# Two blocks on one core: the mixer's last three output tiles and the first two gate and up tiles in token halves, with token sums on TensorE

## Chip, cores and metric

The kernel runs on one core of one Trainium2 chip. The time is that of one execution on the device in microseconds, launch to end, as the median of several runs. Lower is better.

## What is computed

528 tokens of width 1024 (16 meta tokens and 512 of the sequence) go through a first block: a token mixer (a state-space branch and an mLSTM branch, merged) and a gated FFN with a causal convolution along the tokens. A second block, an attention block with its own FFN, follows on the 512 sequence tokens. The change lies where the first block's mixer ends and its FFN begins. All is float32.

```python
def rmsnorm(x, g):
    xf = x.astype(jnp.float32)
    y = xf * lax.rsqrt(jnp.mean(xf * xf, axis=-1, keepdims=True) + NORM_EPS)
    return (y * g.astype(jnp.float32)).astype(x.dtype)

def token_mixer(x, g_pre, g_post, ...):
    ...
    return x + rmsnorm(merged @ w_out, g_post)

def channel_mixer(x, g_pre, g_post, w_gate, w_up, w_conv, b_conv, w_down):
    h = rmsnorm(x, g_pre)
    a = causal_dwconv(h @ w_gate, w_conv, b_conv)
    y = (jax.nn.gelu(a, approximate=True) * (h @ w_up)) @ w_down
    return x + rmsnorm(y, g_post)
```

## The kernel before

Activations lie with features on the 128 partitions and tokens along the free axis; a tile is one of eight blocks of 128 features. The 528 tokens are held as two halves of HF = 258 tokens, from tokens 14 and 270 on (HEADTOK): 256 that count and two ahead of them, which the convolution needs. Each product is made in three matmuls, for accuracy: operands are split into a high and a low part, and `mm3` (L171 to L179) issues, for each block k of the contraction, high by high, high weight by low activation, low weight by high activation, each for every output half. So a tile of 1024 by 128 weights is 48 matmuls for two halves, and a product whose output is one PSUM bank of 512 columns is 24.

`split_w` (L159 to L169) makes the weights ready: SyncE (SP) loads a raw tile (three buffers), ScalarE (ACT) casts it to the high part `wh` (L167), VectorE (DVE) subtracts to get the low part `wl` (L168). High and low parts have four buffers, two in each of two pools that are used in turn.

The place of the change is the end of `token_mixer` (L457 to L498):

1. Eight output tiles (L463 to L468): 48 matmuls each into `d`, two PSUM banks, one for each half; ScalarE copies them to `y` (L467) and squares the copy (L530); GpSimd (POOL) adds the squares up in `nacc` (L534), the last square stays apart as `nsq`.
2. The norm of the output (L470): a token's sum over partitions is a matmul with a vector of ones (`tok_sum`, L210), 128 tokens at a time, five of them for 516 tokens, for `nacc` and for `nsq`; VectorE makes the root in ten small operations (L217, L185 to L195); six transposes (`bcast_cols`, L223) spread it over all partitions. Between them stand matmuls whose results nobody reads ("spins", L230).
3. The residual pass (L472 to L487): for each tile SP loads the input `xr`, VectorE scales each half (`pt`, L478), an add of the input follows (L481, L486; VectorE for even tiles, GpSimd for odd ones), then `part` splits the result into `xh` (ScalarE, L570) and `xl` (VectorE, L571), and its squares are added up (L530, L534).
4. The first FFN tiles, f = 0 and 1 (`ffn_products`, L488): a gate product `fg` of 48 matmuls of 258 columns, an up product `fm` of 24 matmuls of 512 columns.
5. The sums of the second norm, its root, and transposes into the row `ffn_rstd` (L490 to L497). The FFN loop takes the first two tiles' results out of PSUM with it (L1110 `gs`, L1118 `gt`), and from f = 2 on makes its own products.

Which instruction stands where in an engine's queue is set by a scheduler when the kernel is built; the program text gives it the dependences, and `high_priority` and `issue_after` steer it. PSUM has two pools: `pd`, two tiles of two banks (tag `d`), and `pm`, four tiles of one bank (tag `m`).

## Time and profile before

| | us |
|---|---|
| median of 3 runs | 1474.9 (1471.9 to 1474.96) |
| profiled execution | 1474.1 |
| its span, first to last instruction | 1472.3 |
| TensorE busy | 1433.4 (97%) |
| VectorE busy | 818.8 (56%) |
| ScalarE busy | 637.4 (43%) |
| GpSimd busy | 313.8 (21%) |
| mean granted TensorE clock | 0.990 of full speed |

Busy time is that in which an engine has an instruction under way; matmuls overlap, so it is a share of the span in which TensorE is not idle, and not its peak. Weight loads (PEld) are counted apart, since they lie beside matmuls. A start in the timeline is when an instruction began, and the time behind it how long it, or the whole run of like instructions, took; the distance of two starts is the pace. In brackets stands the idle time of the engine ahead of an instruction and what ended it.

### The profile page before, as it was taken

The page shows a single profiled execution, that of the slowest core. Times are in us where ns is not written, and L with a number is a line of the kernel's source. Part 1 is how long each engine was busy: PE and PEld are TensorE (multiplying, and loading weights), DVE is VectorE, ACT ScalarE, POOL GpSimd, SP SyncE. Part 2 cuts the span into 40 slices and gives each one's busy share as a digit, 9 for nine tenths or more (in the row PEclk, how much of TensorE's full clock was granted, in tenths as well). Part 3 has the DMA queues.
Part 4 walks back from the last instruction along what each step waited for, and adds up shares of the span by engine and source line. Part 5 has one row for each costly group of instructions (what it writes and reads, how often), then busy time and mean ns, then how long its engine had stood idle before and what let it go on. Part 6 is the DMA issues. An engine that isn't in the chain of part 4 may idle for free.

```text
span 1472.3 us, 22643 instructions
## 1 busy us (share of the span) xinstructions
PE 1433.4 (97%) x9050; PEld 1294.6 (88%) x9050; DVE 818.8 (56%) x1463; ACT 637.4 (43%) x1026; POOL 313.8 (21%) x383
## 2 busy tenths in 40 slices
PE   7999988999999999999999899999998999999998
PEld 7999988999998988899988799999886888888887
DVE  8868643544447663256543668888776542244321
ACT  4455555732434332233332447777654532134310
POOL 0019881010124210001111513223454000000000
PEclk9999998999999999999999999999999999999999
DMA  5662212232521322332223133333222322222330
GB/s 177 157 116 77 73 65 55 85 94 74 178 91 68 108 85 79 116 101 87 91 80 96 44 105 112 102 109 107 69 70 92 116 92 100 101 93 93 108 122 29
DMA packets 65892, 140.32 MB, mean 95 GB/s; under 512 B 18806, under 2 KB 30454, under 8 KB 65788
## 3 DMA queue, kind: packets, MB, share of 16 engines
q1 hardware_dynamic: 52672, 129.90, 27.2%
q10 hardware_dynamic: 13116, 8.99, 2.6%
q8 instruction: 71, 1.16, 0.3%
q14 instruction: 33, 0.27, 0.1%
HBM read 128.83 MB, written 4.76 MB: 91 GB/s over the span
## 4 chain that ended last, share of the span: by engine, by line
PE 81%; POOL 9%; DVE 4%; issue 2%; ACT 2%; DMA 2%; ACTq 0%; DVEq 0%; POOLq 0%
PE fm L178 16%; PE d L178 13%; PE mp L178 12%; PE ad L178 9%; PE ad L1196 8%; PE fg L178 8%; PE ad L1407 3%; PE ao L178 3%; POOL ra L808 3%; POOL X L810 2%; POOL rb L809 2%; PE at L1317 1%; PE as L1292 1%; PE ao L1329 1%; DVE wl L168 1%
## 5 line engine op out<-in xcount | busy, mean ns | idle before, releaser
L167 ACT CAST wh<-wr 128x1024 fp32r<-128x1024 f32 (+2 forms) x240 | 232.9, 972 | 533.9 <-PE d L178 103.3
L168 DVE TENSOR_TENSOR wl<-wr,wh 128x1024 fp32r<-128x1024 f32 (+2 forms) x240 | 293.4, 1225 | 204.8 <-ACT wh L167 203.3
L178 PE MATMUL d<-xh,wl 128*128 128x258 f32 (+1 forms) x576 | 121.3, 290 | 1.8 <-DVE wl L168 1.8
L178 PE MATMUL d<-xh,wh 128*128 128x258 f32 (+1 forms) x576 | 121.9, 293 | 0.0
L178 PE MATMUL d<-xl,wh 128*128 128x258 f32 (+1 forms) x576 | 119.1, 288 | 0.0
L1196 PE MATMUL ad<-wh,xh 128*128 128x256 f32 x384 | 111.1, 293 | 2.6 <-ACT wh L167 1.3
L1196 PE MATMUL ad<-wh,xl 128*128 128x256 f32 x384 | 111.2, 291 | 1.4 <-DVE xl L571 1.2
L1196 PE MATMUL ad<-wl,xh 128*128 128x256 f32 x384 | 110.6, 290 | 0.4 <-DVE wl L168 0.4
L178 PEld LDWEIGHTS d<-xh,wl 128*128 128x128 f32 x576 | 91.3, 192 | 4.9 <-issue 2.3
L178 PEld LDWEIGHTS d<-xh,wh 128*128 128x128 f32 x576 | 91.8, 194 | 2.6 <-issue 1.0
L178 PEld LDWEIGHTS d<-xl,wh 128*128 128x128 f32 x576 | 91.0, 193 | 0.4
L1119 POOL TENSOR_TENSOR gt<-gt,ga 128x512 f32<-128x512 f32 x22 | 31.5, 1432 | 267.6 <-ACT wh L167 202.9
L1196 PEld LDWEIGHTS ad<-wh,xh 128*128 128x128 f32 x384 | 74.2, 195 | 3.9 <-ACT xh L570 1.9
L1196 PEld LDWEIGHTS ad<-wh,xl 128*128 128x128 f32 x384 | 74.9, 195 | 2.8 <-DVE xl L571 2.2
L1196 PEld LDWEIGHTS ad<-wl,xh 128*128 128x128 f32 x384 | 74.8, 195 | 1.1 <-DVE wl L168 0.7
L178 PE MATMUL fg<-xh,wh 128*128 128x258 f32 x352 | 71.8, 285 | 1.9 <-ACT xh L570 1.9
L534 POOL TENSOR_TENSOR nacc<-nacc,nsq 128x512 f32<-128x512 f32 (+1 forms) x37 | 53.3, 1440 | 91.7 <-ACT nsq L530 88.3
L178 PE MATMUL fg<-xl,wh 128*128 128x258 f32 x352 | 71.7, 286 | 0.7 <-DVE xl L571 0.7
L178 PE MATMUL fg<-xh,wl 128*128 128x258 f32 x352 | 71.9, 285 | 0.0
L178 PE MATMUL fm<-xh,wh 128*128 128x512 f32 x176 | 70.3, 400 | 0.1
L178 PE MATMUL fm<-xl,wh 128*128 128x512 f32 x176 | 70.3, 400 | 0.0
L178 PE MATMUL fm<-xh,wl 128*128 128x512 f32 x176 | 70.0, 397 | 0.0
(459 smaller groups left out, 3622.3 us busy)
## 6 DMA issues: line engine op xcount, KB each, us to landing
wr<-in_wd_dram SPq DMA_DIRECT2D x48, 512.0 KB
wr<-in_wgu_dram SPq DMA_DIRECT2D x44, 512.0 KB
wr<-in_w_dram SPq DMA_DIRECT2D x36, 512.0 KB
wr<-in_wup_dram SPq DMA_DIRECT2D x32, 512.0 KB
wr<-in_wqkv_dram SPq DMA_DIRECT2D x24, 512.0 KB
wr<-in_wo_dram SPq DMA_DIRECT2D x10, 512.0 KB
wr<-in_wab_dram SPq DMA_DIRECT2D x16, 256.0 KB
wr<-in_wd_dram SPq DMA_DIRECT2D x16, 192.0 KB
```

Of the source, the lines that this page charges most:

```text
L167: nc.scalar.copy(hi[:, :n], raw[:, :n])
L168: (eng or nc.vector).tensor_sub(lo[:, :n], raw[:, :n], hi[:, :n].bitcast(F))
L178: self.mm = self.nc.tensor.matmul(o, a[:, k, :], x(k, p), start=first and k == order[0] and t == 0, stop=last and k == order[-1] and t == 2)
L534: self.eng.tensor_add(self.parts[0], self.parts[0], sq)
L808: P.tensor_tensor(a, self.AR, X[:, :, :, k - 1].unsqueeze(1).to_broadcast([128, 2, 2, G]), op=OP.mult)
L809: P.tensor_tensor(b, a[:, 0], a[:, 1, ::-1], op=OP.add)
L810: P.tensor_tensor(X[:, :, :, k], X[:, :, :, k], b, op=OP.add)
L1119: P.tensor_mul(t, t, a)
L1196: nc.tensor.matmul(o, x[:, k, 128 * tt : 128 * tt + 128], w[:, k4], start=k == 0 and i == 0 and tt % 2 == 0, stop=k == 7 and i == 2, skip_ ...
L1292: nc.tensor.matmul(ps[:, b:e], q, kl[:, :n], start=False, stop=True, skip_group_check=True)
L1317: nc.tensor.transpose(pt[:, e : e + 128], p[:, off[i] + 128 * j : off[i] + 128 * j + 128], c.idn)
L1407: nc.tensor.matmul(ps, x[:, k], y[:, k, :S], start=i == 0 and t == 0, stop=i == kt - 1 and t == 2)
```

## The change

Of the eight mixer output tiles, five stay as they are. The last three are made half by half: all three tiles of the first token half, then all three of the second, from the same weights, which stay in their buffers (`ws`). Each half tile is copied, and squared straight from PSUM, on ScalarE. The square of each half tile goes to TensorE by itself: `TokSums.add` issues three sums of 128 tokens (tokens 0, 128 and 130 on) which accumulate in PSUM; the five whole tiles' sum of squares joins them with six sums. The root and the transposes are made for each half.

The residual pass runs by halves too (`residual`): eight tiles of the first half, then eight of the second. Squares of the halves go to TensorE one by one, or in pairs which GpSimd adds first (m = 1, 3, 5); the tiles 1, 3, 5, 6 and 7 give three sums each.

The first two gate and up tiles (`ffn_half`) are made by halves: gate 0, up 0, gate 1, up 1 for the first half, tile by tile; for the second half all four go side by side, k by k. Their four weights stay until the last k. Up products have 256 columns for each half in place of 512. The spins are left out here.

In the sums, L559 of the changed kernel is the matmul of `TokSums.add`, 54 in all: 6, 9 and 9 for the first norm, 15 and 15 for the second.

```diff
-        post = PostNorm(c, op, 2 * HF)
-        for m in range(8):
+        rr = c.xp.tile([128, 2, HF], F, name="ffn_rstd", tag="rrow")
+        thirds = (0, 128, HF - 128)
+
+        def spread(cols):
+            ps = misc()
+            c.bcast_cols(cols, [(j, ps[:, s : s + 128]) for j, s in enumerate(thirds)])
+            return ps[:, :HF]
+
+        def square(x):
+            sq = op.tile([128, HF], F, name="hsq", tag="hsq", bufs=4)
+            A.activation(sq, x, AF.Square)
+            return sq
+
+        post = PostNorm(c, op, 2 * HF, 5, direct=0)
+        for m in range(5):
...
-        pa, pb = misc(), misc()
-        post.finish(misc(), [pa, pb], spins=(4, 8, 6), idle=misc())
+        ws = [c.split_w(I["wo1"][m], 1024) for m in range(5, 8)]
+        sums = TokSums(c, misc())
         pre = PreNorm(c, op, 2 * HF, "g_ffn_pre", 0)
-        for m in range(8):
-            xr = op.tile([128, 2, HF], F, name="xr", tag="xr", bufs=4)
...
-        c.first = [ffn_products(c, f) for f in range(2)]
-        with tc.high_priority():
-            ffn_rstd = pre.finish(misc(), (0, 128, 256, 384, 388))
...
+        def residual(p):
+            for m in range(8):
+                xr = op.tile([128, HF], F, name="xr", tag="xr", bufs=6)
+                nc.sync.dma_start(xr, I["hT"][m][:, HEADTOK[p] : HEADTOK[p] + HF])
+                t = op.tile([128, HF], F, name="pt", tag="pt", bufs=2)
+                V.scalar_tensor_tensor(t, y[:, m, p], c.v("g_mix_post", m), rs[p], op0=OP.mult, op1=OP.mult)
+                (P if m % 2 else V).tensor_add(y[:, m, p], t, xr)
+                pre.part(m, y[:, m], slice(p, p + 1))
+                sq = square(y[:, m, p])
+                if m in (1, 3, 5):
+                    P.tensor_add(sq, sq, last)
+                last = sq
+                if m not in (0, 2, 4):
+                    sums.add(6 + 3 * p, sq, thirds, m == 7)
+
+        def row(p):
+            with tc.high_priority():
+                A.copy(rr[:, p], spread(sums.finish(6 + 3 * p, 3)))
+
+        for p in range(2):
+            if p == 0:
+                sums.add(0, post.parts[0], [HF * q + s for q in range(2) for s in thirds], False)
+            for m in range(5, 8):
...
+                c.mm3([ps], ws[m - 5], 8, lambda k, _: mgh[:, k, p], lambda k, _: mgl[k][:, p])
+                A.copy(y[:, m, p], ps)
+                sums.add(3 * p, square(ps), thirds, m == 7)
+            rs.append(spread(sums.finish(3 * p, 3)))
+            if p == 0:
+                first_weights = [c.split_w(I["wgu"][0, 0], 1024)]
+        residual(0)
+        first_weights += [c.split_w(I["wgu"][f, j], 1024) for f, j in ((0, 1), (1, 0), (1, 1))]
...
+        for j in range(4):
+            outs.append(misc() if j % 2 else c.pd.tile([128, 2, 512], F, name="fg", tag="d"))
+            ffn_half(c, first_weights[j], outs[j], j % 2, 0)
+        row(0)
+        residual(1)
+        for k in range(8):
+            for j in range(4):
+                ffn_half(c, first_weights[j], outs[j], j % 2, 1, (k,))
+        row(1)
...
+class TokSums:
+    def __init__(self, c, ps):
+        self.c, self.ps, self.fresh = c, ps, True
+
+    def add(self, col, a, starts, last):
+        for j, s in enumerate(starts):
+            self.c.nc.tensor.matmul(self.ps[:, col + j : col + j + 1], a[:, s : s + 128], self.c.ones,
+                                    start=self.fresh, stop=last, skip_group_check=True)
+            self.fresh = False
```

How the order moves, at two places. First TensorE (PE) in before, from the last mixer product `d` on (`m` are the one-bank PSUM tiles of sums, transposes and spins):

```order
L178 MATMUL d<-mgh,wl 128x258 x2
L210 MATMUL m<-ones,nacc 128x1 x5
L230 MATMUL m<-idn 128x128 x4
L210 MATMUL m<-ones,nsq 128x1 x5
L230 MATMUL m<-idn 128x128 x8
L223 MATMUL m<-idn,rs_y 128x128 x6
L230 MATMUL m<-idn 128x128 x6
L178 MATMUL fg<-xh,wh 128x258 x3
L178 MATMUL fm<-xh,wh 128x512
```

And TensorE in the changed kernel where the first half's last gate product ends, the second mixer half's root is spread and the up products (`m` of 256 columns) begin:

```order
L178 MATMUL fg<-xh,wh 128x258
L178 MATMUL fg<-xl,wh 128x258
L178 MATMUL fg<-xh,wl 128x258
L559 MATMUL m<-ones,hsq 128x1 x5
L223 MATMUL m<-idn,rs_y 128x128 x3
L559 MATMUL m<-ones,hsq 128x1 x4
L178 MATMUL m<-xh,wh 128x256
L178 MATMUL m<-xl,wh 128x256
L178 MATMUL m<-xh,wl 128x256
```

What stood in one block behind the mixer's last product, with spins between, now stands in pieces among the FFN's products, and the transposes of the second half stand behind the first half's gate products.

Second, VectorE (DVE) in before, where FFN tile 2 begins: `rs_y` is the root of the second norm, `wl` low parts of weights, `gs` and `gt` the reads of the first two gate and up products from PSUM:

```order
L195 SCALAR_TENSOR_TENSOR rs_y<-rs_a,rs_y 128x5
L168 TENSOR_TENSOR wl<-wr,wh 128x1024 x3
L1110 TENSOR_TENSOR gs<-fg,ffn_rstd 128x516
L1118 TENSOR_TENSOR gt<-fm,ffn_rstd 128x512
L1110 TENSOR_TENSOR gs<-fg,ffn_rstd 128x516
L1118 TENSOR_TENSOR gt<-fm,ffn_rstd 128x512
```

The same place on VectorE in the changed kernel:

```order
L195 SCALAR_TENSOR_TENSOR rs_y<-rs_a,rs_y 128x3
L1172 TENSOR_TENSOR gs<-fg,ffn_rstd 128x516
L1180 TENSOR_TENSOR gt<-m,ffn_rstd 128x512
L1172 TENSOR_TENSOR gs<-fg,ffn_rstd 128x516
L1180 TENSOR_TENSOR gt<-m,ffn_rstd 128x512
L168 TENSOR_TENSOR wl<-wr,wh 128x1024 x3
L1176 SCALAR_TENSOR_TENSOR ga<-gs,vec,ga 128x512 x4
```

The three weight remainders for tile 2 stood ahead of the four reads; now they stand behind them.

## Rows read from the trace of the kernel before

**Rows 1.** The page, busy time of each engine, share of the span, instructions.

```profile
PE 1433.4 (97%) x9050; PEld 1294.6 (88%) x9050; DVE 818.8 (56%) x1463; ACT 637.4 (43%) x1026; POOL 313.8 (21%) x383
```

**Rows 2.** TensorE's timeline, mixer products to FFN: start, us, line, operation, out<-in, count.

```profile
380.03 0.40 PE L178 MATMUL d<-mgh,wh 128*128 128x258 f32 x2
...
426.02 0.40 PE L178 MATMUL d<-mgh,wl 128*128 128x258 f32 x2
426.26 1.17 PE L210 MATMUL m<-ones,nacc 128*128 128x1 f32 x10
...
431.69 0.87 PE L223 MATMUL m<-idn,rs_y 128*128 128x128 f32 x6
...
434.87 0.51 PE L178 MATMUL fg<-xh,wh 128*128 128x258 f32 x2 [0.97 <-ACT xh L570]
```

**Rows 3.** Windows: stretch, its us, busy of PE, PEld, DVE, ACT, POOL; clock, DMA.

```profile
434.87:464.11 29.24, 27.47 (x160) 23.85 (x161) 24.83 (x39) 13.07 (x21) 16.75 (x11) 0.94 0.17 51
464.11:812.00 347.89, 347.89 (x1966) 305.23 (x1967) 168.95 (x187) 118.64 (x153) 39.62 (x28) 1.00 0.29 95
438.00:440.00 2.00, 2.00 (x9) 1.72 (x8) 2.00 (x3) 0.09 (x1) 1.96 (x2) 0.50 0.36 108
```

**Rows 4.** Chain of waits, the last pair of residual scalings: start, us, what.

```profile
449.89 0.79 DVE pt L478 x2
```

**Rows 5.** TensorE's timeline in the attention stage, two neighbouring matmuls of 256 columns.

```profile
950.00 0.28 PE L1196 MATMUL ad<-wh,xh 128*128 128x256 f32 x1
950.12 0.28 PE L1196 MATMUL ad<-wh,xl 128*128 128x256 f32 x1
```

**Rows 6.** TensorE's timeline, sums and transposes among the first FFN products.

```profile
457.31 0.40 PE L178 MATMUL fm<-xl,wh 128*128 128x512 f32 x1
457.55 1.17 PE L210 MATMUL m<-ones,nacc 128*128 128x1 f32 x10
458.58 0.48 PE L178 MATMUL fm<-xh,wl 128*128 128x512 f32 x1
458.90 0.41 PE L178 MATMUL fg<-xh,wl 128*128 128x258 f32 x2
...
463.16 0.82 PE L223 MATMUL m<-idn,rs_y 128*128 128x128 f32 x6
```

**Rows 7.** ScalarE's timeline, a weight cast and a half tile's high part.

```profile
426.22 1.05 ACT L167 CAST wh<-wr 128x1024 fp32r<-128x1024 f32 x1 [3.51 <-PE d L178]
...
435.73 0.51 ACT L570 ACTIVATE xh<-x,vec 128x258 fp32r<-128x258 f32 x1 [0.91 <-DVE x L481]
```

**Rows 8.** VectorE's timeline: root, residual pass, weight remainders, reads of PSUM.

```profile
429.85 0.17 DVE L217 TENSOR_SCALAR ms<-m 128x5 f32<-128x5 f32 x1 [1.33 <-PE m L210]
...
432.27 1.66 DVE L478 SCALAR_TENSOR_TENSOR pt<-x,vec,m 128x258 f32<-128x258 f32 x4 [0.64 <-PE m L223]
...
453.55 1.47 DVE L571 SCALAR_TENSOR_TENSOR xl<-x,vec,xh 128x516 fp32r<-128x516 f32 x1 [0.24 <-ACT xh L570]
...
460.46 3.49 DVE L168 TENSOR_TENSOR wl<-wr,wh 128x1024 fp32r<-128x1024 f32 x3
464.42 0.70 DVE L1110 TENSOR_TENSOR gs<-fg,ffn_rstd 128x516 f32<-128x516 f32 x1 [0.47 <-ACT ffn_rstd L497]
...
466.83 1.22 DVE L168 TENSOR_TENSOR wl<-wr,wh 128x1024 fp32r<-128x1024 f32 x1
```

**Rows 9.** Tile pt's instructions, the residual's adds: ns min/median/max, first and last start.

```profile
L486 POOL TENSOR_TENSOR x<-pt,xr x4: 1397/1740/1748, 434.0 to 451.0; 128x516 f32<-128x516 f32 x4
L481 DVE TENSOR_TENSOR x<-pt,xr x2: 420/963/1506, 433.9 to 434.2; 128x258 f32<-128x258 f32 x2
```

**Rows 10.** Groups by form, 408 to 476 us: busy us, mean ns, idle before.

```profile
L571 DVE SCALAR_TENSOR_TENSOR xl<-x,vec,xh 128x258 fp32r<-128x258 f32 x2 | 0.9, 481 | 0.0
```

**Rows 11.** Waits of TensorE, 812 to 1472 us: us in total, times, longest.

```profile
PE ad L178 <- DVE ot L1389: 3.4, 2, 1.7
...
PE ad L178 <- ACT xh L570: 1.2, 1, 1.2
```

More of the change, by code (lines that the diff above doesn't have):

```diff
@@ L468, in mixer @@
             post.add(y[:, m].rearrange("p a b -> p (a b)"))
-        pa, pb = misc(), misc()
-        post.finish(misc(), [pa, pb], spins=(4, 8, 6), idle=misc())
+        ws = [c.split_w(I["wo1"][m], 1024) for m in range(5, 8)]
+        sums = TokSums(c, misc())
         pre = PreNorm(c, op, 2 * HF, "g_ffn_pre", 0)
-        for m in range(8):
-            xr = op.tile([128, 2, HF], F, name="xr", tag="xr", bufs=4)
-            for p in range(2):
-                nc.sync.dma_start(xr[:, p], I["hT"][m][:, HEADTOK[p] : HEADTOK[p] + HF])
-            t = op.tile([128, 2, HF], F, name="pt", tag="pt", bufs=2)
-            for p, ps in enumerate((pa, pb)):
-                V.scalar_tensor_tensor(t[:, p], y[:, m, p], c.v("g_mix_post", m), ps[:, 2 * p : 2 * p + HF],
-                                       op0=OP.mult, op1=OP.mult)
-                if m == 0:
-                    V.tensor_add(y[:, m, p], t[:, p], xr[:, p])
-                    pre.part(m, y[:, m], slice(p, p + 1))
-            if m == 0:
-                pre.add(y[:, m], 2)
-            else:
-                (P if m % 2 else V).tensor_add(y[:, m], t, xr)
-                pre.split(m, y[:, m])
@@ L488, in mixer @@
-        c.first = [ffn_products(c, f) for f in range(2)]
-        with tc.high_priority():
-            ffn_rstd = pre.finish(misc(), (0, 128, 256, 384, 388))
-            rr = c.xp.tile([128, 2, HF], F, name="ffn_rstd", tag="rrow")
-            pa, pb = misc(), misc()
-            c.bcast_cols(ffn_rstd, [(0, pa[:, 0:128]), (1, pa[:, 128:256]), (2, pa[:, 256:384])])
-            c.bcast_cols(ffn_rstd, [(2, pb[:, 0:128]), (3, pb[:, 128:256]), (4, pb[:, 132:260])])
-            rf = rr.rearrange("p a b -> p (a b)")
-            A.copy(rf[:, 0:256], pa[:, 0:256])
-            A.copy(rf[:, 256:516], pb[:, 0:260])
+        rs = []
@@ new lines, in row @@
+        def row(p):
[5 more added lines that the diff above has]
+            for m in range(5, 8):
+                i = 3 * p + m - 5
+                if i % 2 == 0:
+                    pair = dense_ps()
+                ps = pair[:, i % 2, :HF]
+                c.mm3([ps], ws[m - 5], 8, lambda k, _: mgh[:, k, p], lambda k, _: mgl[k][:, p])
[4 more added lines that the diff above has]
+                first_weights = [c.split_w(I["wgu"][0, 0], 1024)]
@@ L498, in mixer @@
+        c.first = [outs[:2], outs[2:]]
     return rr
@@ L513, in weave, with finish @@
             next(once.pop(0))
+class TokSums:
[6 more added lines that the diff above has]
+            self.fresh = False
+    def finish(self, col, n):
+        return self.c.tok_finish(self.ps[:, col : col + n], n)
 class SumSq:
@@ L1068, in res_update, with ffn_half, moving @@
     pre.split(m, x)
+def ffn_half(c, w, out, up, p, ks=range(8)):
+    b = 2 * up
+    o = out[:, 256 * p : 256 * p + 256] if up else out[:, p, :HF]
+    def moving(x):
+        return lambda k, _: x[:, k, 264 * p + b : 264 * p + HF]
+    c.mm3([o], w, 8, moving(c.xh), moving(c.xl), ks[0] == 0, ks[-1] == 7, ks)
 def ffn_products(c, f):
```

1 line of the change is left out of this document (added).

## The prediction

> **What bounds the kernel now.** I read the page's engine line first: TensorE (PE) is busy 97% of the span, and it has as many weight loads as matmuls, 9050 of each [rows 1]. So time can only be won where TensorE waits or does work that the result doesn't need; and that weights "stay" saves no load, since each matmul has its own, whichever order they stand in. Then I read the TensorE timeline from the mixer's last products on [rows 2]. The 384 products run from 380.03 to 426.26 us, 0.1204 us each; then sums, filler matmuls ("spins") and transposes follow, and the first useful product of the FFN starts at 434.87. That is the hole. Behind it TensorE is not at its pace either: the stretch 434.87 to 464.11 had a granted clock of 0.94 [rows 3], and the first four FFN products, 96 x 0.1204 + 48 x 0.24 = 23.1 us of work, lie in 29.2 us. The chain of waits passes through VectorE there [rows 4]: the residual pass. From 464.11, where FFN tile 2 begins, TensorE is busy in every microsecond up to 812 [rows 3]. So one number decides: the time at which the changed kernel begins tile 2, against 464.1. I start at T0 = 380.0 + 5 x 48 x 0.1204 = 408.9, the end of the fifth mixer tile; before takes 55.2 us from there.
>
> **The change: TensorE's work.** (1) Six mixer halves and eight FFN halves are 14 x 24 = 336 matmuls of 256 or 258 columns. Matmuls of this size with a new weight each and one target bank start 0.12 us apart in the attention stage [rows 5], as the pairs did; 336 x 0.1204 = 40.5 us. The up tiles lose their 512-column form, which cost 0.24 (457.31 to 457.55) for twice the columns: no loss. (2) Token sums: 15 before, 54 now. Five of them took 457.55 to 458.58, 1.03 us, so 0.206 each, and the product behind them held TensorE 0.32 us in place of 0.24 [rows 6]: 0.08 for each return to products. 54 x 0.206 + 12 returns x 0.08 = 12.1 us, 8 us of them for 39 more sums. (3) Twelve transposes at 0.82 / 6 = 0.137 [rows 6]: 1.6 us, as many as before. Spins are gone; they filled the hole and cost nothing. Sum: 54.2 us, so with no wait at all tile 2 would begin at 463.1, only **1.0 us** earlier. The hole's idle is bought with sums.
>
> Against that price stands a rule: the Trainium skill's page "TensorE: Matmul & The Clock Gate", section "Back-to-back issue gap", gives 1 to 64 moving columns about 60 cycles, some 25 ns; by that, 54 sums of two matmuls each would be an estimated 2.7 us in place of 11.1, and the sum 45.8. The sums among FFN products [rows 6] decide for 0.206; what cheap sums would give is rival B.
>
> **The waits that stay.** W0: the sum of the second mixer half's second tile waits for its square, which stands on ScalarE behind a weight cast of 1.05 us, a copy and the square itself; a half tile on ScalarE took 0.51 [rows 7], so 2.1 us, covered by some 1.5 us of transposes and sums. I take 0.6; it lies ahead of W1, which swallows it.
> W1: the gate products of the first half need the residual pass. Its start: 86 half matmuls (the order puts 14 of the second half ahead of the sums' end), 15 sums and 3 returns bring the first half's sums to 408.9 + 13.7 = 422.6. The VectorE chain of ten small operations behind them took 1.84 (429.85 to the transposes at 431.69) [rows 2, 8]; it is hidden under the 34 matmuls that the transposes stand behind. They start at 426.7 and VectorE 0.58 later (431.69 to 432.27) [rows 2, 8], at 427.3. TensorE ends the second mixer half at 431.9 (24 matmuls, nine sums, the transposes) and then eats what VectorE delivers. VectorE per half: eight scalings at 0.79 / 2 [rows 4], four adds at 0.42 [rows 9], eight remainders at 0.48 [rows 10], 8.7 us; in the first half also two weight remainders at 3.49 / 3 = 1.16 [rows 8], which stand between them, and in each the small chain of sums, 1.84. From below 12.9 us. From above by the pace of before: 432.27 to 453.55 + 1.47 = 22.75 us for 16 half tiles, 1.42 each [rows 8], because VectorE and GpSimd held each other up (an add of 258 took 0.42 or 1.51 [rows 9]): 15.5. GpSimd's work there goes from eleven operations of 516 to fourteen of 258, so I take the middle, 14.2: the root at 441.5, the last remainder that the gates need 0.9 ahead of it, at 440.6. Behind that remainder stand ten matmuls and five sums, 2.3 us, before the transposes: 442.9, and VectorE's second pass from 443.5. TensorE then has four sums, to 444.2, and the 48 up matmuls, to 450.0, then 22 matmuls with nine sums, to 454.8.
> W2: there the transposes of the first row and the last two sums wait for the end of the second residual pass: 8.7 + 1.84 = 10.5 to 13.2 us, middle 11.9, so 455.4. The wait is a few tenths; the sums end at 456.5. Then 74 matmuls and three transposes, 9.4 us: 465.9.
> W3: weight buffers. The four FFN weights all stay until the last k, so tile 2's casts and remainders can't be made ahead as before, when three remainders were done from 460.46 on, ahead of the four reads of PSUM; now they stand behind these reads. The four took 464.42 to 466.83 = 2.4 us [rows 8], and start 1 us before the products end; with 1.16 for the remainder, tile 2's first low-weight matmul can start 2.5 us after the end, with 1.4 us of work to cover it. W3 = 1.1, at least 0.5 and at most 1.6. Tile 2 starts in earnest at 467.0.
>
> Hidden: the 16 half loads of the residual stand on SP behind weight loads, but each is asked for when a slot of six comes free, two or more tiles ahead; uncovered, one would add its landing to a scaling's add. Copies and squares of the six mixer halves on ScalarE, and the adds on GpSimd: under 24 matmuls each. The squares' adds on GpSimd delay only sums.
>
> Sum: 467.0 - 464.1 = **+2.9 us**; with both ends of the VectorE time +1.6 (tile 2 at 465.7) and +5.2 (469.3). The profiled execution took 1474.1 (span 1472.3), 0.8 below the median of 1474.9; the difference goes on the median: 1477.8, own range 1476.5 to 1480.1. 0.2% is 2.95 us, about what a measurement of this kernel can tell from no change.
>
> **Rivals.**
> A, TensorE-bound: VectorE is quicker than my middle and ScalarE's cast isn't in the way. For it: GpSimd's operations are shorter. Against: even the lower row prices leave W1 and W3. -1.0 to +1.6, middle +0.3: 1475.2.
> B, sums nearly free. Of the 54, those on the way of the chains reach the end: 15 ahead of the first transposes, five behind the last gate remainder, six at the end, 26 x 0.206 = 5.4 us. So -2.5, and +2.9 where VectorE takes over all of it; middle +0.2: 1475.1. The sums' row speaks against it; the page on TensorE named above speaks for it.
> C, the clock. TensorE's granted clock was 0.50 (1.2 GHz) from 438 to 440 [rows 3], after it had waited 0.97 us and run a few single matmuls from 434 on [rows 2]. The new waits come in small pieces between gate products (some 8.7 us of work in 431.9 to 442.9), so I expect it to stay; if it falls for 4 us in the up products, they take 2 us more, and the last pass then comes late by a further 1: 1481.
> D, full lock: VectorE stands still while GpSimd works. If each half's seven GpSimd operations block VectorE for half of the 1.40 that a full one took [rows 9], a half costs 4.9 us more than from below, 17.8 and 15.4, some 3.6 more than I take, in each half: +10, 1485. The Trainium skill's page "SBUF — State Buffer", section "Who interferes with whom", calls the ports that the two share an exclusive lock for a whole instruction, where VectorE reads two SBUF inputs. The add of 1.51 beside GpSimd agrees with it, the one of 0.42 shows that it isn't always met.
> E, the other side, faster: the attention stage. Its order is written anew on all engines too, as far as the scheduler moved rows by some places. TensorE waits there 3.4 us for the attention output and 1.2 us for the products' input [rows 11]. If the new order removes both, 4.6 us go; it decides when the mixer's end loses less than 1.6, that is at my lower end: 1471.9. Against: nothing in the diff aims there, and a moved row can as well add a wait.
>
> **How the numbers follow.** Forecast +1.6 to +5.2: 0.52, of which I put 0.29 above 2.95. A 0.13, B 0.06, C 0.09, D 0.07, E 0.13. Slower: 0.29 + 0.09 + 0.07 = 0.45; same: 0.23 + 0.13 + 0.06 = 0.42; faster 0.13. The range takes in A from -1.0 with a little of E, the forecast, and C with part of D: 1473.3 to 1482.0; left out are most of E and the rest of D.
>
> **What would show it.** Right: no stretch of 8 us without products; tile 2's first 512-column product some 58 us after the fifth mixer tile; 54 sums in 11 us; idle of TensorE on the remainders of the residual (W1, 2 to 3 us) and on the weight remainder or cast at tile 2 (W3, about 1 us); granted clock near 1.00 in the whole stretch. Wrong: sums well under 0.2 us; W1 absent; a clock of 0.5 within; or a difference that lies behind 812, in the attention stage.

## The result, and the profile after

The changed kernel takes 1484.85 us (median, 1482.97 to 1485.88) against 1473.41 (1471.9 to 1474.96) for the kernel before: a ratio of 1.0072, with a 95% interval of 1.006 to 1.0085. It is slower, by about 11 us; +2.9 was forecast, with 1482.0 as the top of the range. (The 1474.9 from which the forecast starts is the median of three of these four runs of before.) Its profiled execution took 1485.88, 11.8 more than that of before, so the two traces can be laid side by side. The page's engine line after, against [rows 1]:

```profile
PE 1444.2 (97%) x9140; PEld 1301.2 (88%) x9140; DVE 824.3 (56%) x1495; ACT 643.5 (43%) x1049; POOL 310.9 (21%) x384
```

TensorE is busy 10.8 us longer with 90 more matmuls. So the loss is mostly work and its pace, and not idle time. To see where, I put the starts of a few TensorE rows side by side, one row for each point at which the program is at the same place in both kernels. TensorE's timeline of before: the first FFN down product, the end of that block, the FFN's sums, the first and the last 512-column product of the second block's FFN (called "the MLP" here), and its last product.

```profile
567.12 0.39 PE L178 MATMUL fm<-ah,wh 128*128 128x512 f32 x1
626.99 0.40 PE L178 MATMUL fg<-xh,wh 128*128 128x258 f32 x2
...
812.62 0.95 PE L210 MATMUL fm<-ones,nacc 128*128 128x1 f32 x8
1140.88 0.50 PE L178 MATMUL mp<-xh,wh 128*128 128x512 f32 x1 [0.67 <-ACT rrow L1152]
...
1456.31 0.39 PE L178 MATMUL mp<-mah,wl 128*128 128x512 f32 x1
...
1468.69 0.28 PE L178 MATMUL mp<-mah,wl 128*128 128x256 f32 x1
```

The same of the changed kernel:

```profile
571.91 0.39 PE L178 MATMUL fm<-ah,wh 128*128 128x512 f32 x1
632.34 0.40 PE L178 MATMUL fg<-xh,wh 128*128 128x258 f32 x2
...
818.53 0.95 PE L210 MATMUL fm<-ones,nacc 128*128 128x1 f32 x8
1149.48 0.50 PE L178 MATMUL mp<-xh,wh 128*128 128x512 f32 x1 [0.67 <-ACT rrow L1214]
...
1468.37 0.39 PE L178 MATMUL mp<-mah,wl 128*128 128x512 f32 x1
...
1480.44 0.28 PE L178 MATMUL mp<-mah,wl 128*128 128x256 f32 x1
```

| from, to | before, us | after, us | difference |
|---|---|---|---|
| first mixer product (380.03; 379.66) to first FFN down product, called "the stretch" below | 187.09 | 192.25 | +5.16 |
| first FFN down product to FFN sums | 245.50 | 246.62 | +1.12 |
| FFN sums to first MLP product | 328.26 | 330.95 | +2.69 |
| first to last 512-column product of the MLP | 315.43 | 318.89 | +3.46 |
| from there to the MLP's last product | 12.38 | 12.07 | -0.31 |

Two things are to be seen. The stretch, which the change is about, loses 5.2 us and not 2.9. And 7.0 us are lost behind it, where the diff touches nothing: one block of 264 FFN down products takes 632.34 - 571.91 = 60.43 us in place of 59.87, and 1391 products of the MLP 318.89 in place of 315.43.

The stretch of before isn't the same in every execution. The traces of e2, e3 and e4 below, whose instructions have the order of before, show 188.8, 187.4 and 188.5 us for it, so against before the change costs 3.5 to 5.2 us there. Each of these four executions also spends 3.4 us of the stretch at a granted clock of 0.50.

Inside the stretch, the windows of the changed kernel (us; busy of PE, PEld, DVE, ACT, POOL; clock; DMA): from the end of the fifth mixer tile to the first gate product, to the second transposes, to the end of the four first products, and the start of tile 2.

```profile
408.69:433.08 24.39, 22.92 (x192) 22.38 (x190) 8.46 (x22) 8.25 (x18) 3.37 (x3) 1.00 0.17 52
433.08:445.01 11.93, 10.36 (x79) 9.19 (x77) 10.24 (x25) 6.69 (x17) 5.78 (x6) 1.00 0.51 161
445.01:467.47 22.46, 22.46 (x193) 22.40 (x192) 13.31 (x44) 7.84 (x20) 6.43 (x7) 1.00 0.05 12
467.47:470.33 2.86, 2.32 (x12) 1.38 (x11) 2.86 (x5) 2.86 (x5) 0.00 (x0) 1.00 0.03 9
```

The granted clock is 1.00 in all four, where before had 0.94 [rows 3]. In the third window TensorE is busy all the time. In the last, 12 matmuls (1.44 us at 0.12) lie in 2.86: W3 is 1.4. TensorE's timeline, at the places that the prediction gave times for:

```profile
414.78 1.39 PE L559 MATMUL m<-ones,nacc 128*128 128x1 f32 x12
416.03 0.81 PE L559 MATMUL m<-ones,hsq 128*128 128x1 f32 x6
420.21 0.83 PE L559 MATMUL m<-ones,hsq 128*128 128x1 f32 x6 [0.75 <-ACT hsq L472]
...
427.39 0.49 PE L223 MATMUL m<-idn,rs_y 128*128 128x128 f32 x3
...
429.44 0.83 PE L559 MATMUL m<-ones,hsq 128*128 128x1 f32 x6 [0.67 <-ACT hsq L472]
...
433.86 0.39 PE L178 MATMUL fg<-xl,wh 128*128 128x258 f32 x1 [0.50 <-DVE xl L622]
...
445.01 0.52 PE L223 MATMUL m<-idn,rs_y 128*128 128x128 f32 x3
...
456.94 1.40 PE L559 MATMUL m<-ones,hsq 128*128 128x1 f32 x12
458.20 0.36 PE L178 MATMUL m<-xl,wh 128*128 128x256 f32 x1
...
467.56 0.51 PE L178 MATMUL fg<-xh,wh 128*128 128x258 f32 x2
```

Six sums take 416.03 - 414.78 = 1.25 us, 0.208 each. TensorE's waits from 405 to 475 us (us in total, times, longest):

```profile
PE fg L178 <- DVE xl L622: 1.5, 4, 0.5
PE m L559 <- ACT hsq L472: 1.4, 2, 0.8
```

### The profile page after: what moved, and what is told of

Same layout as the page of the kernel before. It is cut to its first block, busy times and chain, and to the rows that moved or that the text cites. A ratio compares the mean times of both kernels' runs of the same rounds, so it can differ in the third digit from the quotient of the medians.

```text
span 1484.0 us, 22877 instructions
## 1 busy us (share of the span) xinstructions
PE 1444.2 (97%) x9140; PEld 1301.2 (88%) x9140; DVE 824.3 (56%) x1495; ACT 643.5 (43%) x1049; POOL 310.9 (21%) x384
## 4 chain that ended last, share of the span: by engine, by line
PE 82%; POOL 9%; DVE 3%; issue 2%; ACT 2%; DMA 2%; ACTq 0%; POOLq 0%; DVEq 0%
PE fm L178 16%; PE d L178 13%; PE mp L178 12%; PE ad L178 9%; PE ad L1258 8%; PE fg L178 8%; PE ad L1469 3%; POOL ra L859 3%; PE ao L178 3%; POOL X L861 2%; POOL rb L860 2%; PE at L1379 1%; PE m L178 1%; DVE wl L168 1%; PE as L1354 1%
## 5 line engine op out<-in xcount | busy, mean ns | idle before, releaser
L178 PE MATMUL fm<-ah,wl 128*128 128x512 f32 x176 | 69.0, 394 | 0.0
L178 PE MATMUL fm<-al,wh 128*128 128x512 f32 x176 | 68.7, 392 | 0.0
L178 PE MATMUL fm<-ah,wh 128*128 128x512 f32 x176 | 68.3, 388 | 0.0
L859 POOL TENSOR_TENSOR ra<-AR,X 128x128 f32<-128x128 f32 x64 | 44.0, 687 | 103.4 <-DMA X<-X 98.4
```

The costliest lines, as they stand in the source:

```text
L178: self.mm = self.nc.tensor.matmul(o, a[:, k, :], x(k, p), start=first and k == order[0] and t == 0, stop=last and k == order[-1] and t == 2)
L859: P.tensor_tensor(a, self.AR, X[:, :, :, k - 1].unsqueeze(1).to_broadcast([128, 2, 2, G]), op=OP.mult)
```

## The experiments

All ratios below are against runs of the kernel before that were taken together with the edited kernel, on the same chip; several chips were used, so medians of different sets are compared by their ratios. "Half clock" is a stretch with a granted clock of 0.50 (1.2 GHz).

### Where the time behind the stretch went

The new tiles of the norm's small chain (ms, rs_i, rs_h, rs_a, rs_y in a form of three columns, two buffers each, 32 bytes) take 320 bytes of the pool "small". Everything allocated on that side behind them moves up by 320 bytes: ah from 70208 to 70528, al from 92736 to 93056, the MLP's weights from 148032 to 148352; xh, xl and the first weights stay. The theory: the matmul's pace depends on this place. The rival: the new order of the instructions causes it. L139 has a pad tile in that pool, so the place can be changed alone. e1 gives the changed kernel a pad that makes the move 512 bytes; e2, e3 and e4 move the tiles of the kernel before by 320, 128 and 256 bytes. The instructions and their order on each engine are those of the kernel that was edited.

```diff
-        self.sp.tile([128, 8], F, name="pad", bufs=1)
+        self.sp.tile([128, 56], F, name="pad", bufs=1)
```

(in the changed kernel; for e2 to e4 the width is 88, 40 and 72 in the kernel before; the places named above are those of the built programs)

> Edit: the changed kernel with 192 bytes more in an unused tile of the small pool, so that what lies above it in SBUF sits 512 bytes higher than in the kernel before, not 320. The order on every engine is that of the changed kernel. Theory P (placement): the part of the loss that lies behind FFN tile 2 comes from the 320 bytes by which the new three-column tiles of the norm push everything above them; then matmuls of 512 columns go back to 0.227 us (0.2293 and 0.2316 in two of the three kinds of the FFN's down product now), the second block loses its 5.8 us and the down products 1.1: 1478.0, of which about 4.8 over before remain and belong to the changed stretch. Theory Q (order): the scheduler's new order in the attention stage costs it: 1484.9, no change. Theory R (the whole chip ran slower): no change against the changed kernel, and before of this set is slower too.

> Edit: the kernel before with 320 bytes more in the unused tile of the small pool; order as in before. Theory P: 512-column matmuls of the down products at 0.2293 and 0.2316 us, about 6.9 us lost: 1480.3. Theory Q and theory R: as before, 1473.4.

> Edit: the kernel before with 128 bytes more in the unused tile; order as in before. Theory P with the place counted in steps of 256 bytes: the tiles above lie at 192 in place of 64 and some 3 to 9 us are lost, 1476 to 1482. Theory P with steps of 128 bytes: no change, 1473.4. Theories Q and R: no change.

> Edit: the kernel before with 256 bytes more in the unused tile; order as in before. Theory P with steps of 256 or of 128 bytes: no change, 1473.4, and 0.227 us for each 512-column matmul. If any move costs, or steps are larger than 256: 1476 or more. Theories Q and R: no change.

| run | median (range) | ratio, 95% interval | 264 down products | MLP, 512-column products |
|---|---|---|---|---|
| before | 1474.38 (1471.42 to 1477.32) | | 59.87 | 315.43 |
| after, as it is | 1484.85 (1482.97 to 1485.88) | 1.0072 [1.006, 1.0085] | 60.43 | 318.89 |
| e1: after, moved by 512 | 1483.56 (1478.08 to 1485.96) | 1.0059 [1.004, 1.0078] | 59.87 | 315.43 |
| e2: before, moved by 320 | 1480.73 (1480.03 to 1481.57) | 1.0043 [1.0028, 1.0059] | 60.43 | 318.89 |
| e3: before, moved by 128 | 1482.33 (1482.03 to 1484.21) | 1.0057 [1.0041, 1.0072] | 61.34 | 320.27 |
| e4: before, moved by 256 | 1474.23 (1472.35 to 1479.81) | 1.0003 [0.9991, 1.0014] | 59.87 | 315.43 |

The down block in the timelines of e2 (with its MLP), of e3 and of e4:

```profile
569.83 0.39 PE L178 MATMUL fm<-ah,wh 128*128 128x512 f32 x1
...
630.26 0.40 PE L178 MATMUL fg<-xh,wh 128*128 128x258 f32 x2
...
1145.19 0.50 PE L178 MATMUL mp<-xh,wh 128*128 128x512 f32 x1 [0.68 <-ACT rrow L1152]
...
1464.09 0.39 PE L178 MATMUL mp<-mah,wl 128*128 128x512 f32 x1
```

```profile
566.96 0.39 PE L178 MATMUL fm<-ah,wh 128*128 128x512 f32 x1
...
628.30 0.40 PE L178 MATMUL fg<-xh,wh 128*128 128x258 f32 x2
```

```profile
568.66 0.39 PE L178 MATMUL fm<-ah,wh 128*128 128x512 f32 x1
...
628.53 0.40 PE L178 MATMUL fg<-xh,wh 128*128 128x258 f32 x2
```

And of e1, from its first mixer product on:

```profile
380.19 0.40 PE L178 MATMUL d<-mgh,wh 128*128 128x258 f32 x2
...
572.33 0.39 PE L178 MATMUL fm<-ah,wh 128*128 128x512 f32 x1
...
632.20 0.40 PE L178 MATMUL fg<-xh,wh 128*128 128x258 f32 x2
...
1147.19 0.50 PE L178 MATMUL mp<-xh,wh 128*128 128x512 f32 x1 [0.68 <-ACT rrow L1214]
...
1462.62 0.39 PE L178 MATMUL mp<-mah,wl 128*128 128x512 f32 x1
```

The traces decide it: these two lengths take three pairs of values, and which one depends on the bytes alone. The kernel before, moved by 320, has exactly the lengths of the changed kernel; moved by 256, its own; and the changed kernel, moved on to 512, gets back those of before. A 512-column product of the down block starts 0.2268 us after the last one in the first case, 0.2289 at 320 and 0.2324 at 128; in the MLP it is 0.2268, 0.2293 and 0.2302. In the places, what was moved by 320 or 128 no longer has the remainder 64 in steps of 256 bytes that it had before, and by 256 or 512 it keeps it. Products of 256 and 258 columns took no longer: most kept their 0.12, and those at the end of the MLP, behind its last 512-column product, took 0.31 us less in all at 320.

The price in the trace is 2 x 0.56 (two down blocks) + 3.46 - 0.31 = 4.3 us. The whole kernel lost 6.4 by medians in e2; I had expected 6.9 there. What the trace lacks of that goes with the clock. Every run has a span and a mean granted clock on record, and their product estimates what the run would take without half clock (roughly, since it counts half clock as lost by half, busy or not). Its mean is 1461.3 us for before in this set, 1465.3 for e2, 1469.0 for e3 and 1460.5 for e4: +4.0, +7.7 and -0.8, where the traces have 4.3, 7.7 and 0. By medians the theory P missed on the changed kernel: it gave e1 1478.0, the theory Q 1484.9, and 1483.56 was measured. There too the clock differed between runs, from a span of 1476.2 at 0.995 to 1484.0 at 0.990, and the product gives 1468.2 for e1 and 1470.5 for the changed kernel, 2.3 apart. h3 below repeats the test there with another pair.

The theory Q has a part as well. Behind the FFN, VectorE's instructions come in two orders in all these traces: that of before (in e2, e3 and e4, and below in f5, g3 and h3), and that of the changed kernel (in e1, and below in f1, f2, f3, g1, g2, g4, h1, h2 and i1, so an edit of the mixer's end moves the scheduler from one to the other). From the FFN's sums to the first MLP product the first order took 326.8 to 328.8 us and the second 329.3 to 333.2. Both orders have traces with 10.2 us of half clock in this stage, and these took 328.2 to 328.8 (before, e2, e3, e4, g3, h3) against 329.3 to 329.5 (e1, g1, i1). So the order costs about 1 us in this stage.

### What the sums cost

f3 leaves out 36 of the 54 sums, and with them part of both norms. From here on, all kernels but h3 and i1 are the changed kernel with the pad of e1, so the stretch is compared with 192.14 there.

```diff
-                if m not in (0, 2, 4):
-                    sums.add(6 + 3 * p, sq, thirds, m == 7)
+                if m == 7:
+                    sums.add(6 + 3 * p, sq, thirds, True)
...
-                sums.add(3 * p, square(ps), thirds, m == 7)
+                sq = square(ps)
+                if m == 7:
+                    sums.add(3 * p, sq, thirds, True)
```

> Edit, on the changed kernel with the aligned pad: of the squares only tile 7 of each half (and the five whole tiles) are summed, 18 sums in place of 54; all squares and GpSimd's adds are still made. This leaves out part of both norms. Sums wholly on the path: 36 x 0.206 + some 9 returns x 0.08 = 8.1 us and the waits for squares 1.4, the stretch falls to 183. Sums only where the chains pass (the 26 of the prediction, of which 17 go here): 3.5 us, 188.6. VectorE sets the end: 1 to 2 us, 190.5.

1474.68 (1474.17 to 1478.78), ratio 1.0007 [0.9993, 1.002]; the stretch 187.42, with 3.4 us of half clock in it. So 36 sums were worth 4.7 us on the path, and an estimated 1.5 more without the fall of the clock: nearer to 36 x 0.208 = 7.5 than to nothing. It also shows that without these sums the changed kernel, with the pad, would be no slower than before, and no faster.

f2 takes away 12 sums but keeps the result: GpSimd adds the squares of half tiles 5 and 6 to those of the whole tiles.

```diff
+        nacc = post.parts[0].rearrange("p (a b) -> p a b", a=2)
...
-            if p == 0:
-                sums.add(0, post.parts[0], [HF * q + s for q in range(2) for s in thirds], False)
...
-                sums.add(3 * p, square(ps), thirds, m == 7)
+                sq = square(ps)
+                if m < 7:
+                    P.tensor_add(nacc[:, p], nacc[:, p], sq)
+                else:
+                    sums.add(3 * p, nacc[:, p], thirds, False)
+                    sums.add(3 * p, sq, thirds, True)
```

> Edit, on the changed kernel with the aligned pad: in the first norm GpSimd adds the squares of the half tiles 5 and 6 to the sum of the five whole tiles, as before, and TensorE sums only that and tile 7: 12 sums in place of 24. Theory S (sums cost their 0.206 us each on TensorE's path here, with the waits for squares that they bring): 12 x 0.206 and the 1.4 us of waits for squares go, the stretch falls to 188 to 190. Rival V (VectorE's residual passes set the end, the sums lie beside them): they begin when the transposes come, which is 9 sums earlier at most, but the weight remainder in front stays: 191 to 192. Rival G (GpSimd's adds are late): 192 or more.

It went the other way: 1489.2 (1481.24 to 1491.3), ratio 1.0079 [1.0054, 1.0105], the stretch 200.42. The window of f2 that tells why (columns as above):

```profile
437.30:457.80 20.50, 20.50 (x99) 20.50 (x98) 12.58 (x36) 6.23 (x17) 8.31 (x9) 0.50 0.21 65
```

TensorE is busy in all of these 20.5 us, at half clock. Products of 258 columns start 0.214 us apart there and not 0.120 (438.95 to 439.81 for four), so it costs an estimated 9. Another 3.4 us of half clock begin at 430.5. Ahead of each of the two stands a wait, in f2's TensorE timeline:

```profile
428.93 0.39 PE L178 MATMUL d<-mgh,wh 128*128 128x258 f32 x1 [2.27 <-ACT hsq L472]
...
436.56 0.39 PE L178 MATMUL fg<-xl,wh 128*128 128x258 f32 x1 [1.44 <-DVE xl L626]
```

The first one is new. Two half tiles share one PSUM tile, so the products of a half wait until ScalarE has read the other one out, and ScalarE has a weight cast ahead of that. In the changed kernel the sums stood in that place and filled the time. So the sums are not all waste: in part they keep TensorE going where it would otherwise wait. h1 below takes this wait away with a PSUM tile for each half.

### What the weights that stay cost

f1 runs the second half's products two by two, so that gate 0's and up 0's buffers come free half-way and tile 2's weights can be prepared.

```diff
-        for k in range(8):
-            for j in range(4):
-                ffn_half(c, first_weights[j], outs[j], j % 2, 1, (k,))
+        for pair in ((0, 1), (2, 3)):
+            for k in range(8):
+                for j in pair:
+                    ffn_half(c, first_weights[j], outs[j], j % 2, 1, (k,))
```

> Edit, on the changed kernel with the aligned pad: the second halves of the four FFN products go in two pairs (gate 0 and up 0 block by block, then gate 1 and up 1) in place of all four side by side, so that two of the four weights come free 5.8 us before the end. Measured on the stretch from the first mixer product to the first down product of the FFN, 192.1 us with the aligned pad and 187.1 before. Theory W3 (tile 2 waits because its weights can only be cast and split once all four are read): the stretch falls by the 1.4 us that tile 2 loses at its start, to 190.7. Rival (tile 2 waits for PSUM to be read, or the first pair now waits for the second residual pass): 192 or more.

1479.84 (1477.19 to 1486.32), ratio 1.0039 [1.002, 1.0057]; the stretch 190.68, 1.46 shorter: W3 was there, with the size that the trace of the changed kernel gives it, and this takes it away. In f1's trace two remainders for tile 2 stand on VectorE at 462.60, ahead of the reads of PSUM, as they did in before. The first of these reads comes earlier too, at 464.88, so the waits for weights and for PSUM are not parted by this run.

### What GpSimd costs VectorE

f5 gives the eight adds that GpSimd makes in the residual pass to VectorE, so VectorE has more to do; h3 is the same without the pad.

```diff
-                (P if m % 2 else V).tensor_add(y[:, m, p], t, xr)
+                V.tensor_add(y[:, m, p], t, xr)
```

> Edit, on the changed kernel with the aligned pad: all residual adds on VectorE, none on GpSimd (the squares' adds stay there). Theory L (VectorE and GpSimd hold each other up, adds and remainders take 0.96 us in place of 0.42 and 0.48 beside GpSimd): eight adds at 0.42 cost what four at 0.95 did, the stretch stays at 192 +- 0.7, and the share of VectorE operations of 0.9 us or more falls. Rival (GpSimd's work is free for VectorE): four more adds of 0.42 in each pass, 3.4 us, 195.5.

> Edit: the changed kernel, unaligned as it is, with all residual adds on VectorE. Its twin with the aligned pad took 1476.1 in eight runs that agreed within 3.5 us. Theory P (placement): the down products lose 1.1 and the second block 3.2 to 3.7, so 1480.4 to 1480.9. Rival (in the changed kernel the loss behind tile 2 is the attention stage's order and the clock, not the place): 1476 to 1477.

f5: 1476.11 (1474.39 to 1477.94), ratio 1.0013 [0.9997, 1.0029]; the stretch 190.26, shorter by 1.9 where I expected no more than 0.7 either way. The tile pt's adds of the changed kernel (ns min/median/max, first and last start), and its low parts of the residual from 425 to 460 us (busy us, mean ns, idle ahead):

```profile
L493 POOL TENSOR_TENSOR x<-pt,xr x8: 860/899/1659, 429.4 to 454.2; 128x258 f32<-128x258 f32 x8
L493 DVE TENSOR_TENSOR x<-pt,xr x8: 416/502/970, 430.4 to 453.9; 128x258 f32<-128x258 f32 x8
...
L622 DVE SCALAR_TENSOR_TENSOR xl<-x,vec,xh 128x258 fp32r<-128x258 f32 x16 | 10.0, 629 | 0.0
```

And of f5:

```profile
L493 DVE TENSOR_TENSOR x<-pt,xr x16: 415/422/850, 430.0 to 453.7; 128x258 f32<-128x258 f32 x16
...
L622 DVE SCALAR_TENSOR_TENSOR xl<-x,vec,xh 128x258 fp32r<-128x258 f32 x16 | 7.8, 486 | 0.2 <-ACT xh L621 0.2
```

A low part took 629 ns beside GpSimd's adds and 486 without them, and an add 502 against 422: VectorE was being held up. But low parts and adds together keep it busy for 15.1 us in the changed kernel and for 15.2 in f5, so this alone does not make the stretch 1.9 shorter. GpSimd's own add took 0.90 and VectorE's 0.42, so the chain of a tile is shorter too, and no run parts the two. The whole kernel gained more, 7.4 us by medians against e1: f5 has before's order in the attention stage, and 3.4 us of half clock there where e1 has 10.2.

h3: 1482.79 (1480.5 to 1485.97), ratio 1.0062 [1.0048, 1.0076], and 60.43 and 318.89 for the two lengths. Its program differs from f5 by the pad alone, it was run on another chip, and the two intervals of the ratio are apart, by medians 6.7 us. The place is 4.3 of that in the traces; the rest goes with half clock (h3 has 3.4 us in the stretch and 10.2 in the attention stage, f5 none and 3.4), and span times clock differ by 3.9. So the place of the tiles is shown on the changed kernel too.

i1 makes the same edit of the adds in the kernel before.

> Edit: the kernel before with all residual adds on VectorE, none on GpSimd (placement as before). In before the residual pass took 22.75 us for 16 half tiles, 1.42 each; an add of 516 took 1.79 on VectorE and 1.74 on GpSimd, side by side. If the two held each other up there as in the changed kernel: per whole tile two scalings 0.79, an add some 0.8, a remainder some 0.75, 2.3 us, 18.7 for eight; the first four FFN products end up to 4 us earlier, no earlier than their 23.1 us of work behind 434.9, and the time falls by 2 to 4: 1470 to 1471.5. If GpSimd's work was free for VectorE: four adds more at 0.8 lengthen the pass by 3 us: 1476.

Its stretch is 1.55 shorter (185.54), but the time 1473.3 (1471.12 to 1475.88) against 1474.25, ratio 0.9992 [0.9981, 1.0002]: not to be told from no change. Its attention stage has the changed kernel's order and took 329.30 us for 328.26, which takes back two thirds of it. No version that I ran is clearly faster than the kernel before.

### Both cures together, and fewer sums

g1 has the edits of f1 and f5. g2 adds a high priority for ScalarE's square and copy of each half tile. g3 adds f2's adds on GpSimd, 12 sums fewer. g4 takes also 12 sums of the second norm away, by chained adds on GpSimd.

```diff
+                with tc.high_priority():
+                    sq = square(ps)
+                    A.copy(y[:, m, p], ps)
...
-                if m in (1, 3, 5):
+                if m in (1, 2, 3, 4, 5):
                     P.tensor_add(sq, sq, last)
...
-                if m not in (0, 2, 4):
+                if m > 4:
```

(the first piece is in g2, g3 and g4, the others in g4)

> Edit: aligned pad, second FFN halves in two pairs and all residual adds on VectorE, the two edits together. Same stretch (first mixer product to first down product; 187.1 before, 192.1 aligned). If W3 (1.4 us) and GpSimd's hold on VectorE (1.9 us) lie behind one another: 188.8. If one hides the other: 190.2. Rival C, the clock falls in the stretch as with fewer sums: 195 or more.

> Edit: as the one with pairs and VectorE's adds, and squares and copies of the mixer's half tiles get priority on ScalarE over weight casts. With VectorE keeping up, W0 (TensorE's 0.75 and 0.67 us for squares) is on the path: 188.8 - 1.4 = 187.4. If W0 is still swallowed by a later wait: 188.8. Rival C, clock: 195 or more.

> Edit: as the one before, and GpSimd adds the squares of half tiles 5 and 6, so 12 sums fewer. Sums on the path at 0.206 and some 4 returns at 0.08: 187.4 - 2.8 = 184.6, and 1471 us in all. If it was the late squares that let the clock fall in the earlier run with 12 sums fewer, the priority mends it and the granted clock stays at 1.00; if the sums themselves kept the clock up, it falls again and the stretch takes 193 or more.

> Edit: as the one before, and GpSimd adds up the squares of tiles 0 to 5 in the second norm too (nine sums for each half in place of 15). Sums on the path: 12 x 0.206 + some 3 returns, 2.7 us less, 181.9. If GpSimd's two more adds in each pass hold VectorE up by what they take, or the chain is late: 184 to 186. Rival C, clock: 190 or more.

h1 is g3 with a PSUM tile for each half, so that no half waits for the other's copy; h2 is h1 with all 54 sums and without the priority.

```diff
-                if i % 2 == 0:
-                    pair = dense_ps()
-                ps = pair[:, i % 2, :HF]
+                ps = dense_ps()[:, 0, :HF]
```

> Edit: as the kernel with pairs, VectorE's adds, priority and 12 sums fewer, and each mixer half tile gets a PSUM tile of its own in place of half of a shared pair. Same stretch, 188.7 there (with 3.3 us of TensorE's waits for ScalarE's copies and 3.4 us at half clock), 187.1 before. Theory T (the shared tile makes the next half wait for the copy that stands behind a weight cast): those waits go, and with them the fall of the clock: 188.7 - 1.7 - 3.3 = 183.7, some 3 us less than before in all, 1470 to 1471. If the waits only move to the residual's remainders: 186 to 187, 1473 to 1474.

> Edit: pairs, VectorE's adds and a PSUM tile for each half, with all 54 sums on TensorE and no priority. Stretch: 1.4 us of waits for squares go from the 188.5 (without clock loss) of the kernel with pairs and VectorE's adds: 187.1. Against the kernel with 42 sums this gives the price of 12 sums on the path: 12 x 0.206 and 0.3 of returns, 2.8 us, if they lie on it; nothing if VectorE sets the pace.

| run | median (range) | ratio, 95% interval | stretch | half clock in it |
|---|---|---|---|---|
| g1 | 1478.21 (1475.52 to 1481.66) | 1.0035 [1.0024, 1.0046] | 190.18 | 3.4 us |
| g2 | 1481.87 (1478.92 to 1484.76) | 1.0056 [1.0036, 1.0076] | 190.83 | 3.4 |
| g3 | 1477.39 (1474.71 to 1479.71) | 1.0021 [1.0011, 1.0031] | 188.74 | 3.4 |
| g4 | 1478.75 (1474.37 to 1481.49) | 1.0035 [1.0016, 1.0053] | 189.75 | 6.8 |
| h1 | 1482.08 (1477.13 to 1484.34) | 1.0053 [1.0037, 1.0068] | 189.55 | 10.2 |
| h2 | 1482.75 (1482.11 to 1484.68) | 1.0066 [1.0053, 1.0079] | 192.39 | 10.2 |

With the pace of 0.214 for 0.120, a busy TensorE loses 0.44 of the time at half clock, 1.5 of 3.4 us; in the 10.2 us of h1 and h2 it was busy for 8.5 and 9.3. Less that, the stretches are an estimated 188.7, 189.3, 187.2, 186.8, 185.8 and 188.3, and that of before, with its own 3.4 us, 185.6. The cures add up (192.14 - 1.5 - 1.9 = 188.7 for g1). g4's 12 further sums gave 0.4 where 2.7 was expected, with waits of 0.85 and 1.03 us for low parts in their place. The priority did nothing: its waits for squares are 1.2 us in all. g3's wait for the copy of the other half is 3.3, and h1 removes it. And h2 - h1, two runs with the same length of half clock, and between them 12 sums and the priority that did nothing in g2, gives 2.84 us for 12 sums (2.5 by the estimates), where 2.8 was expected from 0.206 each and the returns.

So without half clock h1 would be level with before in the stretch, and not ahead of it; span times clock says the same of the whole kernel, 1460.7 us for h1 and 1461.5 for before in its set. That h1 is 8 us slower goes with the clock, a mean of 0.987 for 0.993. In h1's TensorE timeline, and in the window that follows:

```profile
435.06 0.58 PE L178 MATMUL fg<-xl,wh 128*128 128x258 f32 x1 [1.78 <-DVE xl L626]
```

```profile
433.30:443.50 10.20, 8.45 (x39) 8.45 (x40) 8.83 (x30) 5.01 (x14) 2.89 (x3) 0.50 0.49 149
```

The half clock begins at 433.3, while TensorE waits 1.78 us for the residual, and lasts until 443.5. All traces here in which TensorE waited for 0.97 us or more at once in this stretch have a fall in it: 0.97 to 1.3 in before [rows 2], e2, e3, e4 and i1, 2.3 in f2, f3, g3 and g4, 1.8 in h1, 1.4 in h2. Where the longest was 0.8, some executions had one (g1, g2, h3) and some none (after, e1, f1, f5). That the wait brings the fall is not shown: in e2, e4 and i1 half clock begins some 5 us ahead of the 0.97 (at 431.2 for 436.6 in e2), and in g1 at 417.5, ahead of its first wait of 0.3 us or more, at 421.0. What differs among these executions isn't settled.

## Why the prediction was wrong

**The step that failed** is "So one number decides: the time at which the changed kernel begins tile 2, against 464.1". It took for granted that everything behind tile 2 keeps its pace. Of the 11.8 us between the traces, 7.0 lie behind it. The 512-column products did not keep their pace: 4.3 us in the trace, and as much in e2 by itself, for small tiles of 320 bytes that neither my sum nor any rival had. The other 2.7 are in the attention stage: 1.1 goes with its new order (e1, whose tiles have their old pace and which has as much half clock there as before, still takes 329.36 us for 328.26), and 1.6 with another 3.4 us of half clock and the tiles' place, which no run parts here. Rival E had looked at that stage, with the wrong sign.

**Inside the stretch** the path was the forecast one and the size wrong: +5.16 for +2.9, at the forecast's own upper end of 5.2. That it ended at the bound is in part luck, since against e2's stretch it would be +3.5. The changed kernel has no half clock there, as forecast, where before has 3.4 us. With the start 0.4 earlier, the terms were, in order:

- W0, the wait of the second half's second sum, was forecast at 0.6 us, swallowed by W1. It was 0.67 (429.44) and swallowed. But the first half has such a wait too, 0.75 at 420.21, which my sum had at nothing: the square of its second half tile stands on ScalarE behind the copy of the third.

```profile
419.50 0.38 ACT L515 COPY x<-d 128x258 f32<-128x258 f32 x1 [4.50 <-PE d L178]
419.77 0.67 ACT L472 ACTIVATE hsq<-d 128x258 f32<-128x258 f32 x2
```

  It lay on the path, since the residual pass hangs on the transposes behind it: they came at 427.39 for 426.7, 0.7 late.
- W1 was larger. VectorE's timeline:

```profile
427.36 1.22 DVE L168 TENSOR_TENSOR wl<-wr,wh 128x1024 fp32r<-128x1024 f32 x1 [2.18 <-ACT wh L167]
428.50 0.87 DVE L492 SCALAR_TENSOR_TENSOR pt<-x,vec,m 128x258 f32<-128x258 f32 x2
429.29 1.22 DVE L168 TENSOR_TENSOR wl<-wr,wh 128x1024 fp32r<-128x1024 f32 x1
...
435.80 1.21 DVE L168 TENSOR_TENSOR wl<-wr,wh 128x1024 fp32r<-128x1024 f32 x1
```

  I had counted two weight remainders; a third one, at 427.36, stands ahead of the first scaling, which so began at 428.50 for 427.3: 1.2 late, 0.7 of it from the wait above. From there to the second transposes (445.01 for 442.9) it took 16.5 us for 15.6, with low parts at 629 ns where I had priced 480. TensorE's own waits for the pass sum to 1.5 us only; VectorE's timeline shows no wait from 427.36 to 443.46.
- W2 and the products behind it took no more than forecast: the products ended at 467.47 for 465.9, 1.6 late, so 0.5 of the 2.1 was made good.
- W3 was 1.4 for 1.1, inside its bounds; f1 removes it.
- The middle that I took for VectorE hid a gain that was to be had: without GpSimd's eight adds the stretch is 1.9 us shorter (f5). So **rival D** was right in kind, and its +10 far too much: the medians of an add are 502 and 422 ns. The Trainium skill's page "SBUF — State Buffer", section "Who interferes with whom", calls the ports that the two engines share an exclusive lock, which a VectorE instruction with two SBUF inputs meets beside a GpSimd instruction that reads SBUF. The longest add of 970 beside GpSimd's adds agrees (850 in f5, where GpSimd still adds squares), and the median shows that most adds met little of it.

**What was right.** "Weights that stay" saved no load: as many loads as matmuls, 9140 of each. A sum cost 0.208 us and 12 of them 2.84 on the path, so the idle of the hole was bought with sums, as the sum of 463.1 said, and f3 shows that with most of them gone, and the pad, the change is worth nothing either way. **Rival B** (sums nearly free) falls with these numbers. By the 25 ns of the Trainium skill's page "TensorE: Matmul & The Clock Gate", section "Back-to-back issue gap", 12 sums of two matmuls would be an estimated 0.6 us; h1 and h2 show 2.84. **Rival C** (the clock) is not in the stretch of the changed kernel, at 1.00 in all four windows; it is in f2, h1 and h2. **Rival A** would have needed a shorter W1, and it was longer.

## What to carry to other kernels

Before costing a change term by term, compare where it puts the buffers: a few new small tiles can move every large one behind them, and the price, here some 4 us in work that the diff doesn't touch, was nearly as large as all that the diff did in its own stretch. A pad tile is a cheap control for that, in the old kernel as in the new. Compare the order of the instructions in stages that the edit doesn't touch, too: the scheduler's other order cost about 1 us here and changed from one experiment to the next. And work that looks like waste on a pacing engine may fill a wait: take it away, and look first at the wait that comes up and at the granted clock of several executions.

## What I had not expected of the hardware

The pace of a 512-column product depends on where its operands stand: 0.2268, 0.2289 and 0.2324 us in the down block with the same instructions, for moves of 0 (or 256, 512), 320 and 128 bytes. Why is not shown; products of 256 and 258 columns took no longer for it. In f2, two waits of 2.3 and 1.4 us in a stretch that was otherwise nearly full came with 23.9 us at half clock, an estimated 10 us lost; in g3, waits of 2.3 and 1.0 came with 3.4 us, 1.5 lost.
